# PEER products of a hybrid decoder block: 32 gated in PSUM and 16 kept in the rings of the split weights, gates stored for 32 tokens at a time

## The chip, the core and the metric

The kernel runs on one core of one Trainium2 chip. The metric is the device time of one execution in microseconds; the kernel before takes 1910.42 us, the median of three runs (1905.02 to 1913.4). Engines: TensorE (PE, its weight loads PEld), VectorE (DVE), ScalarE (ACT), GpSimd (POOL), SyncE (SP), and 16 DMA engines that serve the queues of SP, ACT and POOL.

## The reference

One decoder block for 512 tokens of width 1024: two token mixers (MLA attention and RWKV-7), merged by gates, then PEER, a mixture of 16384 experts, all in fp32. The change touches PEER alone:

```python
q = (h @ w_query).reshape(B, S, 8, 2, 128)
s1 = einsum('bshd,nd->bshn', q[..., 0, :], sub_keys1)      # 128 row keys
s2 = einsum('bshd,nd->bshn', q[..., 1, :], sub_keys2)      # 128 column keys
...                                                        # top 16 of each, then top 16 of their sums
expert_idx = i1 * 128 + i2                                 # 16 experts for each of 8 heads
gates = softmax(top_v)
act = gelu(einsum('bpd,bphkd->bphk', h_blk, expert_down[idx]))
out = einsum('bphk,bphkd->bpd', gates * act, expert_up[idx])
```

So a token has 128 experts of 16384. The result is x + gt2 * out.

## The kernel before

The 512 tokens are four blocks of 128. After the token mixers (RWKV in chunks, MLA, `tail_a` to `tail_c`, which end with the query products `ps_q`, the scores `ps_sc` and the selection `select`), the blocks go two ways. Blocks 0 and 1 are **gathered** (`peer`, L1141): for each of the 128 slots an indirect DMA of POOL brings one expert row for each token (`gl`, 128 x 2048, 1 MB, four buffers), VectorE makes the dot product with the token (`gl`, L1156), ACT the gelu and the gate (`z`), and VectorE adds the weighted second half to `acc` (L1163), one slot later, which frees the buffer. Between block 0 and block 1, `acc` is stored and cleared again by POOL.

Blocks 2 and 3 (256 tokens) are **dense**: all 16384 experts are computed for them, 128 at a time; i is the row key, 0 to 127. `dense_z(i)` (L1202) multiplies the 128 down weights `u_raw` with the tokens, 128 x 256 results, and applies the gelu. It has two forms. Made ahead of the loop, it takes the weights as they are, as eight fp32 products with `hf`, which the trace shows as 16 passes. In the loop it splits the weights into a high part `uh` (ACT) and a low part `ul` (VectorE) of a faster format and makes 24 products with the split tokens `hh` and `hl`. `uh` and `ul` have two buffers each.

Before the change 24 products (`AF_`) are made into `Af`, 8 more (up to `AZ` = 32) into a tile `A`, and 8 more (`PZ`) into `zp`, which ACT stores to DRAM as `zd`; the loop loads them again into the first slots of `Af`.

`dense_spread` (L1241) turns the selected experts into gates. For eight tokens (`HB`) VectorE makes one-hots of the row and column keys in 16-bit (`o`, four of 1024 elements at a time) and weights them with the gates (`og`); TensorE multiplies them (`ps_G`), which gives for each token a 128 x 128 table, four tokens in one PSUM bank. VectorE multiplies the first `AF_` rows straight into `Af` out of PSUM (L1290); ACT copies the other rows into `g_` (L1288), and one DMA of ACT's queue stores `g_` to DRAM as `gd` for every `TB` = 16 tokens (L1291). `g_` and the gate tiles `G` that the loop loads back share `NG` = 3 buffers. ahead["z"] is stepped once for each 16 tokens, so 16 products are made during the spread.

The loop of `dense` (L1314) goes over i. It loads the up weights `v_raw`, splits them (`vh`, `vl`), multiplies `act` by the gates `G` if i >= `AF_` (L1334), splits the product (`ch`, `cl`) and adds 12 products of 512 columns to four PSUM accumulators. `gates_of` loads `G` for eight rows i at a time. All products, copies and splits go through the helpers of L237 and L1187 to L1188.

What sets the order: the program is written stage by stage, and a scheduler gives each engine one fixed order by data readiness, a cost model and a priority. `tc.cur_priority += LATE` marks the gather steps and `ZLATE` the products made ahead as work for gaps. So the gathers of both blocks lie between the instructions of all stages from 470 us on.

Of the kernel before, what the change touches and what calls it, by code (L numbers as in the profile page):

```python
# [9 lines left out]
F32 = mybir.dt.float32  # L10
# [25 lines left out]
ZLATE = 100  # L36
ZFIRST = 24
AZ = 32
AF_ = 24
PZ = 8  # L40
NG = 3
BG = [[0.91, 2, 2, 1.0, 2.2, 2.85, 2.45, 1.0], [1.6, 2.28, 1, 0.58, 0.25, 0.5, 0.13, 0.36]]
# [114 lines left out]
def _build(ctx, tc, nc, A, out):  # L157
# [1017 lines left out]

    TB = 16
    HB = 8
# [3 lines left out]
    dn, ahead = {}, {}  # L1181
    zd = dp.tile([P, PZ, nd], F32, name="zd")
    NJ = P // SUB - AF_ // SUB
# [18 lines left out]
    def dense_z(i):  # L1202
# [3 lines left out]
        if i < AF_:  # L1206
            act = dn["first"][:, i]
        elif i < AZ:
            if i % SUB == 0:
                dn["A"] = dz.tile([P, SUB, nd], F32, name="A", tag="A", bufs=(AZ - AF_) // SUB)  # L1210
            act = dn["A"][:, i % SUB]
        elif i < AZ + PZ:
            act = dz.tile([P, nd], F32, name="zp", tag="zp", bufs=2)
        else:
            act = dn["v"].tile([P, nd], F32, name="act", tag="act", bufs=2)
        u = dz.tile([P, D], F32, name="u_raw", tag="u", bufs=4)
        nc.sync.dma_start(u, A["dense"][i, 0])
        if i < AZ + PZ:
            zs = ((u, dn["hf"]),)
# [10 lines left out]
        S.activation(act, ps[:, :nd], AF.Gelu_apprx_tanh)  # L1230
        if AZ <= i < AZ + PZ:
            nc.scalar.dma_start(zd[:, i - AZ], act)
        else:
            dn["act"][i] = act

    def dense_ahead():
        for i in range(AZ + PZ):
            dense_z(i)
            yield
# [54 lines left out]
    def dense(sel):  # L1294

        n = nd
        for _ in dense_spread(sel):
            step(ahead["z"])
        drain(ahead["z"])
# [14 lines left out]
        for i in range(P + 1):  # L1314
            if i < P:
                if i % SUB == 0:
                    if i >= AF_:
                        gates_of(i // SUB + NG - 1)
                    if AZ <= i + SUB < AZ + PZ:
                        t = dn["first"][:, i + SUB - AZ:i + 2 * SUB - AZ]  # L1320
                        nc.sync.dma_start(t, zd[:, i + SUB - AZ:i + 2 * SUB - AZ])
                        for j in range(SUB):
                            dn["act"][i + SUB + j] = t[:, j]
                if i >= AZ + PZ:
                    dense_z(i)
# [147 lines left out]
    for _ in streams[1]:  # L1473
        if "z" in ahead and nz < ZFIRST:
            tc.cur_priority += ZLATE
# [30 lines left out]
```

## Time and profile before

| what | before |
|---|---|
| median of three runs | 1910.42 us |
| the profiled execution | 1907.93 us, of which 1906.2 us is the span of the trace |
| TensorE busy | 1720.0 us (90%) |
| VectorE busy | 1587.9 us (83%) |
| ScalarE, GpSimd busy | 699.8 us (37%), 437.2 us (23%) |
| bytes moved | 588.75 MB, 309 GB/s over the span |

The stages of the end of the span: the last query scores are made by 1081 us, the selection of blocks 2 and 3 ends at 1126, the spread lasts from 1126 to 1247, the dense loop from 1248 to 1872, and the gathers of block 1 end at 1900. A timeline row gives start and duration in us, and in square brackets how long the engine stood idle before it and what ended that. [...]

### The profile page before, as it was taken

How to read it: one execution, taken by the hardware profiler on the slowest of the kernel's cores; microseconds unless marked ns; L12 is line 12 of the kernel's file. 1: busy time of each engine (PE TensorE's matmuls, PEld its weight loads, DVE VectorE, ACT ScalarE, POOL GpSimd, SP SyncE). 2: the span in 40 equal slices, each digit the busy share in tenths (PEclk: the TensorE clock that was granted, in tenths of full speed). 3: DMA queues.
4: the chain of work that ended last, by engine and by line, in shares of the span. 5: the costliest groups of instructions: out<-in, count | busy, mean ns of one | idle time of the engine just before them, and what ended most of it. 6: DMA issues, size and time to landing. Idle time of an engine off the chain costs nothing.

```text
span 1906.2 us, 30258 instructions
## 1 busy us (share of the span) xinstructions
PE 1720.0 (90%) x11018; PEld 1472.0 (77%) x11018; DVE 1587.9 (83%) x3654; ACT 699.8 (37%) x1727; POOL 437.2 (23%) x394
## 2 busy tenths in 40 slices
PE   5879999999899999999699979779999999999992
PEld 4667877778787698988388868657899988889892
DVE  4864446559778798888689999979999999999998
ACT  1233233321323232331131133335555555555551
POOL 1210010000222210222222222022333333333333
PEclk9889999999999999999899989879999999999996
DMA  9545654166986875889899889989999999999997
GB/s 385 196 154 172 230 174 161 44 217 204 365 333 211 345 247 190 298 312 362 330 351 351 317 302 316 293 330 399 400 403 416 415 416 415 414 408 415 411 373 281
DMA packets 146274, 588.75 MB, mean 309 GB/s; under 512 B 13886, under 2 KB 41918, under 8 KB 111564
## 3 DMA queue, kind: packets, MB, share of 16 engines
q1 hardware_dynamic: 76544, 284.69, 40.4%
q0 software_dynamic: 39360, 280.51, 38.2%
q10 hardware_dynamic: 30220, 21.60, 3.6%
q8 instruction: 87, 1.43, 0.3%
q14 instruction: 63, 0.52, 0.1%
HBM read 566.81 MB, written 19.94 MB: 308 GB/s over the span
## 4 chain that ended last, share of the span: by engine, by line
issue 31%; PE 31%; DVE 13%; POOL 12%; DMA 11%; ACT 1%; POOLq 0%; SPq 0%; ACTq 0%; DVEq 0%
POOL gl L1152 12%; DMA gl<-in_experts,ii 5%; PE ps_b L237 4%; PE ps_gt L237 4%; DMA w_b<-in_w_b 3%; PE ps_q L237 3%; DVE acc L1163 3%; PE ps_z L237 2%; DVE gl L1156 2%; PE ps_ap L237 2%; PE ps_y L237 1%; PE ps_m L237 1%; PE ps_G L237 1%; PE ps_M L237 1%; PE ps_s L237 1%
## 5 line engine op out<-in xcount | busy, mean ns | idle before, releaser
L1152 POOL DMA_INDIRECT gl<-in_experts,ii x256 | 382.9, 1496 | 989.1 <-DVE acc L1163 697.0
L1156 DVE SCALAR_TENSOR_TENSOR gl<-gl,h2p 128x1024 f32<-128x1024 f32 x256 | 311.3, 1216 | 49.8 <-DMA gl<-in_experts,ii 49.5
L1163 DVE SCALAR_TENSOR_TENSOR acc<-gl,z,acc 128x1024 f32<-128x1024 f32 x256 | 326.6, 1276 | 12.6 <-ACT z L1158 7.1
L237 PE MATMUL acc<-vl,ch 128*128 128x512 f32 x512 | 204.9, 400 | 7.4 <-DVE vl L1188 7.2
L237 PE MATMUL acc<-vh,cl 128*128 128x512 f32 x512 | 204.5, 399 | 5.0 <-DVE cl L1188 4.9
L237 PE MATMUL ps_z<-hh,uh 128*128 128x256 f32 x704 | 199.4, 283 | 0.0
L237 PE MATMUL ps_z<-hh,ul 128*128 128x256 f32 x704 | 199.4, 283 | 0.0
L237 PE MATMUL acc<-vh,ch 128*128 128x512 f32 x512 | 196.9, 397 | 2.7 <-ACT ch L1187 2.7
L237 PE MATMUL ps_z<-hl,uh 128*128 128x256 f32 x704 | 199.2, 283 | 0.0
L1157 ACT ACTIVATE z<-z 128x1 f32<-128x1 f32 x256 | 51.8, 203 | 368.0 <-DVE gl L1156 367.2
L237 PE MATMUL ps_z<-hf,u_raw 128*128 128x256 f32 x640 | 156.0, 388 | 8.4 <-ACT i1T L1264 8.4
L1188 DVE TENSOR_TENSOR vl<-v_raw,vh 128x1024 fp32r<-128x1024 f32 x128 | 156.0, 1219 | 4.6 <-ACT vh L1187 4.4
L237 PE MATMUL ps_gt<-hT,w_b 128*128 128x128 f32 x1024 | 136.9, 288 | 14.5 <-DMA w_b<-in_w_b 14.4
L237 PEld LDWEIGHTS ps_gt<-hT,w_b 128*128 128x128 f32 x1024 | 127.6, 201 | 20.9 <-DMA w_b<-in_w_b 11.5
L237 PEld LDWEIGHTS ps_z<-hl,uh 128*128 128x128 f32 x704 | 135.1, 192 | 3.8
L1187 ACT CAST vh<-v_raw 128x1024 fp32r<-128x1024 f32 x128 | 134.1, 1047 | 9.6 <-PE acc L237 4.8
L237 PEld LDWEIGHTS ps_z<-hh,uh 128*128 128x128 f32 x704 | 134.7, 191 | 3.4
L237 PEld LDWEIGHTS ps_z<-hh,ul 128*128 128x128 f32 x704 | 134.8, 191 | 0.3 <-DVE ul L1188 0.2
L237 PEld LDWEIGHTS ps_z<-hf,u_raw 128*128 128x128 f32 x640 | 117.1, 194 | 21.8 <-ACT i1T L1264 8.6
L237 PE MATMUL ps_b<-hT,w_b 128*128 128x128 f32 x896 | 123.6, 288 | 7.7 <-DMA w_b<-in_w_b 6.4
L237 PE MATMUL ps_q<-h2T,w_q 128*128 128x128 f32 x1024 | 125.6, 277 | 2.1 <-DMA w_q<-in_w_query 1.4
L237 PEld LDWEIGHTS ps_b<-hT,w_b 128*128 128x128 f32 x896 | 113.3, 200 | 18.0 <-DMA w_b<-in_w_b 6.3
(445 smaller groups left out, 3299.3 us busy)
## 6 DMA issues: line engine op xcount, KB each, us to landing
u_raw<-in_dense SPq DMA_DIRECT2D x128, 512.0 KB, 7.4
v_raw<-in_dense SPq DMA_DIRECT2D x128, 512.0 KB, 8.7
w_b<-in_w_b SPq DMA_DIRECT2D x82, 512.0 KB, 4.8
w_ada<-in_w_ada SPq DMA_DIRECT2D x48, 512.0 KB, 5.4
w_q<-in_w_query SPq DMA_DIRECT2D x48, 512.0 KB, 3.7
G<-gd SPq DMA_DIRECT2D x13, 1024.0 KB, 10.6
w_o<-in_w_o SPq DMA_DIRECT2D x24, 512.0 KB, 5.1
w_out<-in_w_out SPq DMA_DIRECT2D x24, 512.0 KB, 7.0
```

What stands on the lines that cost most here:

```text
L237: PE.matmul(o, l, r, start=start, stop=stop)
L1152: G.indirect_dma_start(out=gl, out_offset=None, in_=A["experts"], in_offset=bass.IndirectOffsetOnAxis(ap=ii[:, s:s + 1], axis=0))
L1156: V.scalar_tensor_tensor(gl[:, :D], gl[:, :D], 1.0, h2, op0=ALU.mult, op1=ALU.mult, accum_out=z[:, 0:1])
L1157: S.activation(z[:, 1:2], z[:, 0:1], AF.Gelu_apprx_tanh)
L1163: V.scalar_tensor_tensor(acc, gl[:, D:], z[:, 1:2], acc, op0=ALU.mult, op1=ALU.add)
L1187: S.copy(hi, x)
L1188: V.tensor_tensor(lo, x, hi.bitcast(F32), op=ALU.subtract)
```

## The change

`AF_` becomes 32, so `Af` has 32 rows and 32 rows of the gate table meet their products in PSUM; `A` and `AZ` go. The 16 products of i = 32 to 47 (`PZ`) go into tiles `zp` of four products each, which take the two `uh` buffers (32 to 39) and the two `ul` buffers (40 to 47); the loop reads them there, and `zd` goes. The first split weights of the loop are those of i = 48, which need `zp` read up to 43. `TB` becomes 32, `NG` 2, and `gd` has 12 groups of rows (`NJ`) and not 13, so 8 stores of 1536 runs of 1 KB take the place of 16 stores of 1664 runs of 512 B. ahead["z"] is stepped twice for each 32 tokens.

```diff
-ZFIRST = 24
-AZ = 32
-AF_ = 24
-PZ = 8
-NG = 3
+AF_ = 32
+PZ = 16
+NG = 2
...
-    TB = 16
+    TB = 32
...
-    zd = dp.tile([P, PZ, nd], F32, name="zd")
     NJ = P // SUB - AF_ // SUB
...
         if i < AF_:
             act = dn["first"][:, i]
-        elif i < AZ:
-            if i % SUB == 0:
-                dn["A"] = dz.tile([P, SUB, nd], F32, name="A", tag="A", bufs=(AZ - AF_) // SUB)
-            act = dn["A"][:, i % SUB]
-        elif i < AZ + PZ:
-            act = dz.tile([P, nd], F32, name="zp", tag="zp", bufs=2)
+        elif i < AF_ + PZ:
+            if i % 4 == 0:
+                tag = ("uh", "ul")[(i - AF_) // 8]
+                dn["zp"] = dz.tile([P, 4, nd], F32, name="zp", tag=tag, bufs=2)
+            act = dn["zp"][:, i % 4]
         else:
...
-        if i < AZ + PZ:
+        if i < AF_ + PZ:
             zs = ((u, dn["hf"]),)
...
-        if AZ <= i < AZ + PZ:
-            nc.scalar.dma_start(zd[:, i - AZ], act)
-        else:
-            dn["act"][i] = act
+        dn["act"][i] = act
...
         for _ in dense_spread(sel):
-            step(ahead["z"])
+            step(ahead["z"], 2)
...
-                    if AZ <= i + SUB < AZ + PZ:
-                        t = dn["first"][:, i + SUB - AZ:i + 2 * SUB - AZ]
-                        nc.sync.dma_start(t, zd[:, i + SUB - AZ:i + 2 * SUB - AZ])
-                        for j in range(SUB):
-                            dn["act"][i + SUB + j] = t[:, j]
-                if i >= AZ + PZ:
+                if i >= AF_ + PZ:
                     dense_z(i)
...
-        if "z" in ahead and nz < ZFIRST:
+        if "z" in ahead and nz < AF_:
```

The scheduler places everything anew from the end of the selection on; up to there VectorE's order is the same. At three places the orders are shown.

TensorE between the last scores (`ps_sc`) and the first gate table (`ps_G`); `ps_igT` are the transposes of the selection that the one-hots need, one row of `ps_z` is two passes in the trace. Before:

```order
L237 MATMUL ps_sc<-sk,qTp 128x128 x4
L237 MATMUL ps_z<-hf,u_raw 128x256 x71
L1263 MATMUL ps_igT<-cst,idx_8605 128x128
L237 MATMUL ps_z<-hf,u_raw 128x256 x3
L1263 MATMUL ps_igT<-cst,idx_8605 128x128
L237 MATMUL ps_z<-hf,u_raw 128x256 x4
L1263 MATMUL ps_igT<-cst,gates_8552 128x128
L237 MATMUL ps_z<-hf,u_raw 128x256 x6
L237 LDWEIGHTS o_8742
```

After:

```order
L235 MATMUL ps_sc<-sk,qTp 128x128 x4
L235 MATMUL ps_z<-hf,u_raw 128x256 x135
L1256 MATMUL ps_igT<-cst,idx_8604 128x128 x2
L235 MATMUL ps_z<-hf,u_raw 128x256
L1256 MATMUL ps_igT<-cst,gates_8551 128x128
L235 MATMUL ps_z<-hf,u_raw 128x256 x6
L235 LDWEIGHTS o_8837
```

The 64 products of eight more rows i stand ahead of the transposes.

VectorE at the start of the spread, from the last steps of the selection (`oh`, `idx`) to the first multiplication out of PSUM. Before:

```order
L1119 TENSOR_TENSOR oh<-oh 128x256
L1266 TENSOR_TENSOR gT<-gT,gb 128x128
L1120 TENSOR_TENSOR idx_8697<-oh 128x128
L1267 CAST gb<-gT 128x128
L1276 TENSOR_TENSOR o_8742<-iota,i2T 128x1024
L1276 TENSOR_TENSOR o_8743<-iota,i1T 128x1024
L1276 TENSOR_TENSOR o_8771<-iota,i2T 128x1024
L1279 TENSOR_TENSOR og<-o_8743,gb 128x1024 x2
L1163 SCALAR_TENSOR_TENSOR acc<-gl,z,acc 128x1024
L1276 TENSOR_TENSOR o_8772<-iota,i1T 128x1024
L1290 SCALAR_TENSOR_TENSOR Af<-Af,ps_G 128x24x4
```

After, from the same `oh` to the first one-hot (a seventh `gl` follows it, ahead of the first row of L1283):

```order
L1117 TENSOR_TENSOR oh<-oh 128x256
L1154 SCALAR_TENSOR_TENSOR gl,z<-gl,h2p 128x1024
L1118 TENSOR_TENSOR idx_8744<-oh 128x128
L1161 SCALAR_TENSOR_TENSOR acc<-gl,z,acc 128x1024
L1154 SCALAR_TENSOR_TENSOR gl,z<-gl,h2p 128x1024
L1161 SCALAR_TENSOR_TENSOR acc<-gl,z,acc 128x1024 x2
L1154 SCALAR_TENSOR_TENSOR gl,z<-gl,h2p 128x1024
L1161 SCALAR_TENSOR_TENSOR acc<-gl,z,acc 128x1024
L1154 SCALAR_TENSOR_TENSOR gl,z<-gl,h2p 128x1024
L1161 SCALAR_TENSOR_TENSOR acc<-gl,z,acc 128x1024
L1154 SCALAR_TENSOR_TENSOR gl,z<-gl,h2p 128x1024
```

Seven gathers moved ahead of the first gate. Counted over VectorE's whole order, 128 of the 256 `gl` stood ahead of the first `vl` before and 135 stand there now; behind the last `vl` there were 9 and are 6; the five `ul` of the spread are gone from it, and the first `ul` follows the 44th `vl`.

VectorE from the last multiplication out of PSUM to the first one by a loaded `G`, after the change (before, it read `Af`, `vl`, the end of block 0's `acc`, three `gl`, `acc` and four splits, and then `A<-A,G`):

```order
L1283 SCALAR_TENSOR_TENSOR Af<-Af,ps_G 128x32x4
L1185 TENSOR_TENSOR vl<-v_raw,vh 128x1024
L1161 SCALAR_TENSOR_TENSOR acc<-gl,z,acc 128x1024
L1154 SCALAR_TENSOR_TENSOR gl,z<-gl,h2p 128x1024 x2
L1185 TENSOR_TENSOR cl<-Af,ch 128x256
L1185 TENSOR_TENSOR vl<-v_raw,vh 128x1024
L1185 TENSOR_TENSOR cl<-Af,ch 128x256
L1161 SCALAR_TENSOR_TENSOR acc<-gl,z,acc 128x1024
L1154 SCALAR_TENSOR_TENSOR gl,z<-gl,h2p 128x1024
L1161 SCALAR_TENSOR_TENSOR acc<-gl,z,acc 128x1024
L1185 TENSOR_TENSOR vl<-v_raw,vh 128x1024
L1322 SCALAR_TENSOR_TENSOR zp<-zp,G 128x256
```

The end of block 0 (`acc<-acc,e`) moved from here into the spread.

## Rows read from the trace of the kernel before

**Rows 1.** Page, part 1: engine, busy us (share of the span), instructions.
```profile
PE 1720.0 (90%) x11018; PEld 1472.0 (77%) x11018; DVE 1587.9 (83%) x3654; ACT 699.8 (37%) x1727; POOL 437.2 (23%) x394
```
**Rows 2.** Two stretches: us, busy us of each engine, TensorE's clock, DMA, GB/s.
```profile
1250.00:1300.00 50.00, 41.91 (x153) 32.45 (x154) 38.25 (x63) 19.36 (x36) 8.65 (x6) 0.85 0.95 372
...
1500.00:1600.00 100.00, 99.70 (x637) 89.81 (x636) 98.07 (x131) 54.65 (x110) 34.52 (x21) 1.00 1.02 415
```
**Rows 3.** Waits from 1310 to 1870 us: us in total, times, longest.
```profile
POOL gl L1152 <- DVE acc L1163: 369.1, 111, 5.6
...
DVE gl L1156 <- DMA gl<-in_experts,ii: 6.5, 12, 1.2
```
**Rows 4.** TensorE's timeline in the dense loop: start us, duration us, instruction.
```profile
1500.45 0.40 PE L237 MATMUL acc<-vh,cl 128*128 128x512 f32 x1
1500.68 0.28 PE L237 MATMUL ps_z<-hh,uh 128*128 128x256 f32 x1
1500.80 0.28 PE L237 MATMUL ps_z<-hl,uh 128*128 128x256 f32 x1
```
**Rows 5.** VectorE's groups, 1310 to 1860 us: busy us, mean ns, idle before.
```profile
L1188 DVE TENSOR_TENSOR ul<-u_raw,uh 128x1024 fp32r<-128x1024 f32 x83 | 101.6, 1224 | 0.1
...
L1334 DVE SCALAR_TENSOR_TENSOR act<-act,G 128x256 f32<-128x256 f32 x84 | 34.9, 415 | 0.0
```
**Rows 6.** TensorE's timeline between the last scores and the spread.
```profile
1080.74 30.59 PE L237 MATMUL ps_z<-hf,u_raw 128*128 128x256 f32 x141
...
1124.74 4.49 PE L237 MATMUL ps_z<-hf,u_raw 128*128 128x256 f32 x12 [8.39 <-ACT i1T L1264]
```
**Rows 7.** VectorE's timeline: the first one-hot and the first gate.
```profile
1126.52 0.68 DVE L1276 TENSOR_TENSOR o<-iota,i2T 128x1024 f16<-128x1024 f16 x1
...
1131.33 0.24 DVE L1290 SCALAR_TENSOR_TENSOR Af<-Af,ps_G 128x96 f32<-128x96 f32 x1
```
**Rows 8.** POOL's and VectorE's timelines, two gathers: issue, then first use.
```profile
906.05 1.68 POOL L1152 DMA_INDIRECT gl<-in_experts,ii  x1 [4.07 <-DVE acc L1163]
...
915.53 1.23 DVE L1156 SCALAR_TENSOR_TENSOR gl<-gl,h2p 128x1024 f32<-128x1024 f32 x1 [3.74 <-DMA gl<-in_experts,ii]
...
1878.12 1.68 POOL L1152 DMA_INDIRECT gl<-in_experts,ii  x1 [6.21 <-DVE acc L1163]
...
1884.53 1.23 DVE L1156 SCALAR_TENSOR_TENSOR gl<-gl,h2p 128x1024 f32<-128x1024 f32 x1 [0.60 <-DMA gl<-in_experts,ii]
```
**Rows 9.** VectorE's groups, 1125 to 1250 us: the multiplications out of PSUM.
```profile
L1290 DVE SCALAR_TENSOR_TENSOR Af<-Af,ps_G 128x96 f32<-128x96 f32 x64 | 14.3, 246 | 2.9 <-ACT g__9404 L1288 1.7 <-ACT g__9700 L1288 0.4 <-ACT g__9774 L1288 0.4
```
**Rows 10.** Last gate store (op, ns, start), and SP's wait for it (total, times, longest).
```profile
L1291 ACTq DMA_DIRECT2D gd<-g__9848 x1: 521/521/521, 1246.9 to 1246.9; - x1
...
SPq L1307 <- DMA gd<-g__9848: 10.8, 1, 10.8
```
**Rows 11.** VectorE's timeline: last gate, and the loop's first waits.
```profile
1247.42 0.25 DVE L1290 SCALAR_TENSOR_TENSOR Af<-Af,ps_G 128x96 f32<-128x96 f32 x1
...
1260.36 1.28 DVE L1163 SCALAR_TENSOR_TENSOR acc<-gl,z,acc 128x1024 f32<-128x1024 f32 x1 [4.96 <-POOL acc L1147]
...
1266.37 0.43 DVE L1334 SCALAR_TENSOR_TENSOR A<-A,G 128x256 f32<-128x256 f32 x1 [3.25 <-DMA G<-gd]
1266.71 0.42 DVE L1188 TENSOR_TENSOR cl<-Af,ch 128x256 fp32r<-128x256 f32 x1
```
**Rows 12.** POOL's timeline: a gather's issue in the spread.
```profile
1213.87 4.42 POOL L1152 DMA_INDIRECT gl<-in_experts,ii  x1 [25.08 <-DVE Af L1290]
```
**Rows 13.** VectorE's timeline: the last `vl`, and the last gathers.
```profile
1865.28 1.22 DVE L1188 TENSOR_TENSOR vl<-v_raw,vh 128x1024 fp32r<-128x1024 f32 x1
1866.41 1.27 DVE L1163 SCALAR_TENSOR_TENSOR acc<-gl,z,acc 128x1024 f32<-128x1024 f32 x1
...
1895.58 1.28 DVE L1163 SCALAR_TENSOR_TENSOR acc<-gl,z,acc 128x1024 f32<-128x1024 f32 x1 [0.60 <-ACT z L1158]
...
1898.60 1.28 DVE L1163 SCALAR_TENSOR_TENSOR acc<-gl,z,acc 128x1024 f32<-128x1024 f32 x1 [0.60 <-ACT z L1158]
```

More of the change, by code (lines that the diff above doesn't have):

```diff
@@ L1230, in dense_z @@
         S.activation(act, ps[:, :nd], AF.Gelu_apprx_tanh)
-        if AZ <= i < AZ + PZ:
-            nc.scalar.dma_start(zd[:, i - AZ], act)
-        else:
-            dn["act"][i] = act
+        dn["act"][i] = act
     def dense_ahead():
-        for i in range(AZ + PZ):
+        for i in range(AF_ + PZ):
             dense_z(i)
```

## Prediction

> **What bounds the kernel now.** First the busy times: TensorE and VectorE hold 90% and 83% of the span [rows 1], so the stages have to be looked at one by one. The change works on the last 830 us. Cut into stretches, the dense loop runs with VectorE at 98.07 of 100 us, TensorE at 99.70 and the DMA engines full at 415 GB/s, while its first 50 us have VectorE at 38.25 of 50 and a granted TensorE clock of 0.85, a mean of time at 1.2 and at 2.4 GHz [rows 2]. Next, who waits for whom in that loop: the gathers on POOL wait 369.1 us for VectorE's `acc`, which frees their buffers, and VectorE waits only 6.5 us for gathered data [rows 3]. So VectorE is never without work there; DMA is full without yet being late. TensorE is no looser: a 512-column product starts 0.23 us after the one before it, a 256-column one 0.12 us [rows 4], so one round (12 of the first, 24 of the second) needs 12 x 0.23 + 24 x 0.12 = 5.64 us, and no gap stands between them. Last, the end: VectorE splits the last `vl` at 1865.28 and is busy with left-over gathers up to the last `acc` at 1898.60, 7.6 us before the span ends [rows 13]. VectorE's last gather ends the kernel, hence VectorE's work and its idle time from 1125 us on are the sum to make; TensorE is checked against it.
>
> **VectorE's work.** Eight products move from the split form to the fp32 form ahead of the loop. Each drops one `ul` of 1.22 us [rows 5]; the next instruction starts 0.08 us before such a one is over (1865.28 to 1866.41 [rows 13]), so 8 x 1.13 = 9.0 us go. Eight more groups of products (24 to 31) meet their gates in PSUM and drop the multiplication by `G`, 0.34 us from start to start (1266.37 is followed by 1266.71, as the 0.42 of [rows 5] less the same overlap): 8 x 0.34 = 2.7 us. Against that, the 64 multiplications out of PSUM grow from 96 to 128 elements. 96 take 246 ns [rows 9], 256 take 415 [rows 5]: 1.06 ns for an element, 64 x 32 x 1.06 = 2.2 us more. Work: -9.0 - 2.7 + 2.2 = **-9.5 us**. Gathers are only moved: one costs 1.14 + 1.20 = 2.34 us wherever it stands (a `gl` of 1.23 [rows 8] and an `acc` of 1.28 [rows 13], less the same overlap).
>
> **The start of the spread.** Before, VectorE goes from selection straight to the first one-hot at 1126.52 and the first gate at 1131.33 [rows 7]. The new order puts seven gathers ahead of the first gate, because 32 products must now be there and not 24. TensorE needs 30.59 / 141 = 0.217 us for a pass of an fp32 product, 16 passes = 3.47 us, and 8 more are 27.8 us; it stood idle for 8.39 us at this place [rows 6], the rest lies beside VectorE's seven gathers (7 x 2.34 = 16.4 us). The products are thus hidden; were the cover gone, each would cost 3.47. What I charge is the wait for gathered data. Four buffers exist, and two full ones stand ready. The third gather can start only when the first `acc` frees a buffer, near 1127. Where gathers stood close together, one issued at 906.05 was waited for until 915.53, 9.5 us; at the quiet end, issued at 1878.12, it was there at 1884.53, 6.4 us [rows 8]. With 9.5 us VectorE waits until 1136.7 though it would be ready near 1133, and the next ones follow at 2.5 to 3.5 us: 5 us lost. If the products' weights (0.52 MB per 3.47 us, 150 GB/s) leave only 265 of 415 GB/s, a gather of 1.05 MB takes 4 us and 9 us are lost. With 6.4 us almost nothing is. I take **+7**, between the two readings of the crowded row that it resembles; bounds 0 and 12.
>
> **Inside the spread.** VectorE idled 2.9 us before its PSUM multiplications, for ACT's copies of `g_` [rows 9]. ACT loses five `uh` casts, eight stores of `zp` and half of its gate stores there, so I take **-2**; at best -2.9, and the other end is the rival below.
>
> **The start of the loop.** VectorE lost 4.96 us to the clearing of `acc` behind the store of the first gathered block, and 3.25 us to the first `G` [rows 11]. The seven gathers let the first block end inside the spread, so the first wait goes. What is late next: in the new order two `gl` and one `acc` stand directly behind the spread, and the second `gl` has its buffer freed only 5 us ahead: with 9.5 us to land it waits 4. The first `G` has to wait for the last store, which was issued at 1246.9 and made the load queue wait 10.8 us [rows 10]. That store has 1536 runs now (1664 before), of 1 KB and not 512 B. Priced by runs it takes as long as before, and VectorE, whose order reaches the `G` some 16 us after the last gate (18.95 before, 1247.42 to 1266.37 [rows 11]), waits 1 to 5 us; by bytes (x1.85) the 14.6 us from issue to release become 27, and it waits 16. Queued behind that wait are the `v_raw` loads on SP and the first `cl`. I take runs: **0** for this place in all, bounds -8 and +11.
> On this the Trainium skill's "DMA: Bandwidth & Descriptors" (Queues, rings and completion order) says that an engine serves the queues in turn, a packet at a time; by that rule the run count decides beside busy queues. No row separates runs from bytes, as all stores here are alike.
>
> The Trainium skill's "SBUF — State Buffer" (SBUF: two separate sides) says that GpSimd cannot write gather descriptors while VectorE holds the shared port in a two-port mode. Its trace sign is here: a gather's issue on POOL takes 4.42 us beside the 16-bit one-hots [rows 12] and 1.68 away from them [rows 8]. By the rule a gather wanted right behind the spread lands 2.7 us later still, which would turn the 0 of the last step into +3.
>
> **The end.** Behind the last `vl` the order has three gathers fewer. In that tail every `gl` and `acc` pair waits about 0.6 us for ACT between them (one gather in 3.02 us, 1895.58 to 1898.60 [rows 13]), so three gathers fewer are up to 3 x 0.6 = 1.8 us of waits fewer; **-1.5**, bounds -3 and +2 (a landing of 9.5 and not 6.4 us there [rows 8]).
>
> **Sum**: -9.5 + 7 - 2 + 0 - 1.5 = -6.0 us. The profiled execution took 1907.93 us around a span of 1906.2; it lies 2.5 below the median 1910.42. So 1901.9 for such an execution, **1904** for a median (-0.3%). TensorE's check: its loop falls from 128 x 2.76 + 85 x 2.88 = 598 us (three split products were made in the spread) to 128 x 2.76 + 80 x 2.88 = 584, and starts later by 16.4 + 7 less what the spread saves (five `ul` of 1.13, 2.0 of idle, 2.2 back, 5.5 in all), 18 us. It would end 4 us later, with three gathers of 3 us fewer behind it: -5. The two ways agree.
>
> **Rivals.** (a) *The work comes through whole.* The DMA load falls (2 MB of `zd`, 2 MB of gates, 14,000 runs), gathers land in the 6.4 us of the quiet row, and the vanished 4.96 us are not replaced: -9.5 + 1 - 2.9 - 4 - 1.5 = -17, so 1893; with half of it 1899. For it: VectorE waits 6.5 us for data in a loop with DMA full [rows 3], so data is rarely late. Against it: [rows 8], where gathers stand as close as they will. (b) *The two gate buffers bind, slower.* Group g+2 of 32 tokens copies into the buffer of group g, whose store must be over: some 14.5 us of time, as long as three buffers of 16 tokens gave. Priced by bytes a store takes 27 us in company; VectorE's gate needs ACT's copy [rows 9], so six groups wait. It decides from 14.5 us a store; at 18 it costs 6 x 3.5 = 21 and 5 at the loop's start, -6 + 26 = +20: 1930. Against it: three buffers were enough under a fuller DMA, and with runs the price is nil. (c) *The change does not remove the stall it moves.* The products wait in the rings of `uh` and `ul`, so the first split waits for product 43 and the loop starts on split products with none in hand, where five `ul` were done by the spread's end. If TensorE, as tight as VectorE [rows 2], has to wait there for three rounds' products (3 x 2.88 = 8.6), the time is 1910 to 1913.
>
> **Chances.** About 0.5%, 9.6 us, is what a measurement of this kernel can tell from no change. The forecast 1901 to 1908: 0.44; (a) 1889 to 1900: 0.36; (b) 1920 to 1940: 0.12; (c): 0.08. Faster 0.36, same 0.51 (forecast and most of (c)), slower 0.13. The range 1890 to 1915 leaves out most of (b) and the far edge of (a).
>
> **What would show it.** `ul` 80 times and the multiplications by `G` 96 times; the PSUM ones near 0.28 us. The first one-hot near 1146 and the first gate near 1153; waits of 5 to 9 us for gathers ahead of it. No wait of ACT for `gd`. The last gate near 1265, no wait on POOL's clearing of `acc`, the first `G` with a wait of 1 to 5 us. The last `vl` near 1867 and 6 gathers behind it. I am wrong by (a) if the waits before the first gate are under 2 us, by (b) if ACT's copies wait for stores, by (c) if TensorE idles where `act` begins.

## The result and the profile after

The changed kernel takes 1895.1 us (median of ten runs, 1887.16 to 1899.35) against 1910.0 (ten runs, 1898.86 to 1913.4): a ratio of 0.9922, 95% interval 0.9903 to 0.9942. It is faster by 0.8%, some 15 us. The forecast was 1904 with a range of 1890 to 1915: the time lies inside, the sign is right, and the gain is two and a half times the 6 us that were worked out.

| | before | after |
|---|---|---|
| the profiled execution, and its span | 1907.93, 1906.2 us | 1887.16, 1885.4 us |
| TensorE busy | 1720.0 us | 1715.8 us |
| VectorE busy | 1587.9 us | 1577.7 us |
| bytes moved | 588.75 MB | 584.53 MB |

The line of the page on busy times, after (as [rows 1] before):

```profile
PE 1715.8 (91%) x10954; PEld 1467.6 (78%) x10954; DVE 1577.7 (84%) x3638; ACT 690.7 (37%) x1719; POOL 422.8 (22%) x394
```

The spans differ by 20.8 us and the medians by 14.9. The cast of `iota`, an instruction of VectorE at the selection's end, up to which both orders are the same, starts at 1125.11 before and at 1118.38 after; 6.7 us thus lie ahead of the change. A second profiled execution of the changed kernel has it at 1130.49. So everything below is measured from that cast. From there to the end of the span it is 781.09 us before, and 767.02 and 768.61 in the two executions after: 14.1 and 12.5 us fewer, which agrees with the medians.

Stretches of VectorE's time: from the cast to the first gate, the spread, from the last gate to the first multiplication by `G`, from there to the last `vl`, the tail. The columns are us, then busy us of PE, PEld, DVE, ACT and POOL, TensorE's clock, DMA share, GB/s. Before:

```profile
1125.11:1131.33 6.22, 6.22 (x34) 5.12 (x34) 6.22 (x15) 1.06 (x3) 0.26 (x1) 0.76 0.61 193
1131.33:1247.42 116.09, 99.38 (x811) 84.42 (x809) 112.28 (x221) 43.96 (x103) 25.46 (x9) 0.91 0.94 303
1247.42:1266.37 18.95, 13.06 (x37) 9.10 (x37) 10.60 (x17) 7.52 (x18) 4.30 (x3) 0.73 0.90 322
1266.37:1865.28 598.91, 591.79 (x3517) 521.41 (x3518) 586.87 (x783) 327.46 (x644) 194.69 (x116) 0.99 1.01 405
1865.28:1906.20 40.92, 5.85 (x24) 3.87 (x22) 33.30 (x44) 5.64 (x22) 12.47 (x8) 0.63 0.77 280
```

After:

```profile
1118.38:1147.90 29.52, 22.24 (x103) 18.13 (x102) 23.31 (x37) 6.44 (x24) 8.57 (x7) 0.83 0.90 365
1147.90:1258.20 110.30, 94.45 (x745) 78.56 (x743) 107.39 (x213) 37.78 (x96) 11.16 (x10) 0.86 0.78 279
1258.20:1276.30 18.10, 11.31 (x35) 8.09 (x36) 11.99 (x18) 6.14 (x16) 4.29 (x3) 0.70 1.01 365
1276.30:1855.00 578.70, 574.15 (x3402) 507.31 (x3401) 571.80 (x760) 322.53 (x631) 190.04 (x112) 1.00 1.01 406
1855.00:1885.40 30.40, 5.62 (x23) 3.69 (x21) 24.73 (x33) 3.30 (x14) 7.06 (x4) 0.69 0.70 259
```

The reader is to take from each row its length less DVE's busy time, which is VectorE's idle time there: 0, 3.8, 8.4, 12.0 and 7.6 us before (31.8 in all), 6.2, 2.9, 6.1, 6.9 and 5.7 after (27.8). VectorE's work from the cast on is 749.3 us before and 739.2 after. The gain of 14.1 us is 10.0 us of work and 4.0 of idle time.

VectorE's timeline at the start of the spread, after (start, duration, instruction, in brackets the idle time and what ended it):

```profile
1128.41 1.23 DVE L1154 SCALAR_TENSOR_TENSOR gl<-gl,h2p 128x1024 f32<-128x1024 f32 x1 [1.74 <-DMA gl<-in_experts,ii]
...
1130.24 1.28 DVE L1161 SCALAR_TENSOR_TENSOR acc<-gl,z,acc 128x1024 f32<-128x1024 f32 x1 [0.60 <-ACT z L1156]
...
1132.80 1.23 DVE L1154 SCALAR_TENSOR_TENSOR gl<-gl,h2p 128x1024 f32<-128x1024 f32 x1 [1.27 <-DMA gl<-in_experts,ii]
...
1140.32 1.23 DVE L1154 SCALAR_TENSOR_TENSOR gl<-gl,h2p 128x1024 f32<-128x1024 f32 x1 [0.65 <-DMA gl<-in_experts,ii]
1141.47 0.08 DVE L1154 DVE_READ_ACCUMULATOR gl<-gl,h2p 128x1 f32 x1
1141.47 0.69 DVE L1269 TENSOR_TENSOR o<-iota,i1T 128x1024 f16<-128x1024 f16 x1
```

The gathers moved ahead are waited for in small pieces: 4.3 us for their data and three times 0.6 for ACT's gate between `gl` and `acc`. The same view at the loop's start, after (as [rows 11] before):

```profile
1263.40 1.23 DVE L1154 SCALAR_TENSOR_TENSOR gl<-gl,h2p 128x1024 f32<-128x1024 f32 x1 [1.29 <-DMA gl<-in_experts,ii]
...
1270.26 1.23 DVE L1154 SCALAR_TENSOR_TENSOR gl<-gl,h2p 128x1024 f32<-128x1024 f32 x1 [2.62 <-DMA gl<-in_experts,ii]
...
1276.30 0.42 DVE L1322 SCALAR_TENSOR_TENSOR zp<-zp,G 128x256 f32<-128x256 f32 x1 [2.14 <-DMA G<-gd]
...
1283.54 0.42 DVE L1185 TENSOR_TENSOR cl<-Af,ch 128x256 fp32r<-128x256 f32 x1 [1.19 <-ACT ch L1184]
```

The wait for the clearing of `acc` is gone, the second gather is waited for in its place, and the wait for `G` is a little shorter.

### The profile page after: what moved, and what is told of

Read it like the earlier page. It is cut to its first block, busy times and chain, and to the rows that moved or that the text cites. A ratio compares the mean times of both kernels' runs of the same rounds, so it can differ in the third digit from the quotient of the medians.

```text
span 1885.4 us, 30072 instructions
## 1 busy us (share of the span) xinstructions
PE 1715.8 (91%) x10954; PEld 1467.6 (78%) x10954; DVE 1577.7 (84%) x3638; ACT 690.7 (37%) x1719; POOL 422.8 (22%) x394
## 2 busy tenths in 40 slices
DMA packets 130369, 584.53 MB, mean 310 GB/s; under 512 B 13598, under 2 KB 26270, under 8 KB 95916
## 4 chain that ended last, share of the span: by engine, by line
PE 32%; issue 27%; DVE 15%; DMA 14%; POOL 12%; ACT 1%; SPq 0%; POOLq 0%; DVEq 0%; ACTq 0%
POOL gl L1150 12%; DMA gl<-in_experts,ii 6%; PE ps_b L235 4%; PE ps_gt L235 4%; PE ps_q L235 3%; DMA w_b<-in_w_b 3%; DMA w_ada<-in_w_ada 3%; PE ps_ap L235 3%; DVE gl L1154 2%; DVE acc L1161 2%; PE ps_y L235 1%; PE ps_z L235 1%; PE ps_m L235 1%; PE ps_sq L235 1%; DVE og L1272 1%
## 5 line engine op out<-in xcount | busy, mean ns | idle before, releaser
L1150 POOL DMA_INDIRECT gl<-in_experts,ii x256 | 368.4, 1439 | 997.8 <-DVE acc L1161 707.4
L1161 DVE SCALAR_TENSOR_TENSOR acc<-gl,z,acc 128x1024 f32<-128x1024 f32 x256 | 326.3, 1275 | 6.1 <-ACT z L1156 5.4
L235 PE MATMUL ps_z<-hf,u_raw 128*128 128x256 f32 x768 | 185.0, 388 | 3.9 <-DMA u_raw<-in_dense 3.9
L235 PE MATMUL ps_z<-hh,ul 128*128 128x256 f32 x640 | 181.1, 283 | 0.0
L235 PE MATMUL ps_z<-hh,uh 128*128 128x256 f32 x640 | 181.0, 283 | 0.0
L235 PE MATMUL ps_z<-hl,uh 128*128 128x256 f32 x640 | 181.0, 283 | 0.0
L235 PEld LDWEIGHTS ps_z<-hf,u_raw 128*128 128x128 f32 x768 | 141.2, 193 | 20.8 <-issue 4.5
L235 PE MATMUL ps_gt<-hT,w_b 128*128 128x128 f32 x1024 | 132.7, 283 | 12.9 <-DMA w_b<-in_w_b 12.7
L235 PEld LDWEIGHTS ps_q<-h2T,w_q 128*128 128x128 f32 x1024 | 122.1, 192 | 4.6 <-ACT h2T L1022 1.5
L235 PEld LDWEIGHTS ps_z<-hl,uh 128*128 128x128 f32 x640 | 122.9, 192 | 3.5
L235 PEld LDWEIGHTS ps_z<-hh,uh 128*128 128x128 f32 x640 | 122.5, 191 | 3.1
## 6 DMA issues: line engine op xcount, KB each, us to landing
G<-gd SPq DMA_DIRECT2D x12, 1024.0 KB, 10.4
```

The source lines that it names most:

```text
L235: PE.matmul(o, l, r, start=start, stop=stop)
L1150: G.indirect_dma_start(out=gl, out_offset=None, in_=A["experts"], in_offset=bass.IndirectOffsetOnAxis(ap=ii[:, s:s + 1], axis=0))
L1161: V.scalar_tensor_tensor(acc, gl[:, D:], z[:, 1:2], acc, op0=ALU.mult, op1=ALU.add)
```

## Experiments

From here on theory V says that the end is set by VectorE's work from the cast on plus its waits; its rivals put the end down to TensorE's rounds, to the DMA engines, or to the gate buffers. All runs in one table: the ratio to the kernel before, run on the same chip (medians 1909.8 to 1911.2), with its interval, and from one profiled execution each, the time from the cast to the end of the span, VectorE's work in it, and its idle time. Work and idle time add up to the time in any kernel; that they do is no evidence for V.

| kernel | products ahead | median us | ratio | cast to end | work | idle |
|---|---|---|---|---|---|---|
| before | 40 | 1910.0 | 1 | 781.1 | 749.3 | 31.8 |
| changed | 48 | 1895.1 | 0.9922 [0.9903, 0.9942] | 767.0 | 739.2 | 27.8 |
| changed_again | 48 | 1899.3 | 0.9926 [0.9900, 0.9952] | 768.6 | 740.3 | 28.3 |
| gates_only | 40 | 1923.7 | 1.0079 [1.0047, 1.0111] | 796.3 | 750.1 | 46.2 |
| gates_early | 40 | 1926.3 | 1.0081 [1.0054, 1.0107] | 791.0 | 750.2 | 40.8 |
| af24 | 40 | 1908.7 | 0.9986 [0.9960, 1.0012] | 778.0 | 749.3 | 28.6 |
| pz8 | 40 | 1908.9 | 0.9997 [0.9972, 1.0023] | 781.7 | 749.2 | 32.6 |
| no_gates | 48 | 1912.4 | 1.0005 [0.9980, 1.0030] | 782.8 | 740.6 | 42.2 |
| no_gates_late | 48 | 1906.8 | 0.9979 [0.9950, 1.0009] | 782.2 | 740.6 | 41.7 |
| igt_first | 48 | 1903.3 | 0.9964 [0.9937, 0.9992] | 777.5 | 740.5 | 37.0 |
| u5 | 48 | 1893.1 | 0.9903 [0.9874, 0.9931] | 766.2 | 739.9 | 26.4 |
| pz20 | 52 | 1889.8 | 0.9900 [0.9862, 0.9937] | 762.9 | 734.9 | 27.9 |
| less_pe | 48 | 1911.7 | 1.0006 [0.9983, 1.0030] | 787.8 | 741.6 | 46.2 |
| more_dma | 48 | 1932.7 | 1.0122 [1.0073, 1.0171] | 766.4 | 739.8 | 26.6 |

**The parts alone.** gates_only is the kernel before with the stores of the change:

```diff
-NG = 3
+NG = 2
-    TB = 16
+    TB = 32
-            step(ahead["z"])
+            step(ahead["z"], 2)
```

> The kernel before with only the gate stores changed: 32 tokens a store, two buffers, 8 stores of 1 KB runs; products and split weights as before. Theory V (the end is VectorE's work plus its waits): VectorE's work stays the same, only its waits for ACT's copies can shrink, so about 1909 us (1905 to 1912), ratio to before 0.997 to 1.001. Theory D (the DMA engines' time decides): half the runs are gone, q10 falls from about 35% to 25% of the engines' time in 135 us, so up to 13 us are gained: 1897 to 1902. Theory B (two gate buffers bind): ACT's copies wait for stores, 1920 or more, and the trace shows it.

It came out at 1923.7, slower than before by 0.8%. Theory V as put here and theory D both missed; B's number came, but hardly by its mechanism: ACT waits once for a gate buffer, 4.8 us, and VectorE waits for ACT's copies for 0.9 us in all. VectorE's work is that of before, and the idle time grew by 14.4 us, most of it at one place, as its timeline at the loop's start shows:

```profile
1258.63 1.23 DVE L1156 SCALAR_TENSOR_TENSOR gl<-gl,h2p 128x1024 f32<-128x1024 f32 x1 [10.37 <-DMA h2p<-h2d]
...
1271.71 1.22 DVE L1169 TENSOR_TENSOR acc<-acc,e 128x1024 f32<-128x1024 f32 x1
...
1288.55 1.23 DVE L1156 SCALAR_TENSOR_TENSOR gl<-gl,h2p 128x1024 f32<-128x1024 f32 x1 [7.87 <-DMA gl<-in_experts,ii]
```

The order that the scheduler makes with the new stores has the end of block 0 (`acc<-acc,e`) among the loop's first rounds. There VectorE waits 10.4 us for the next block's `h2p` and 7.9 for a gather, which POOL could issue only when `acc` was done. Before the change the end of block 0 stood at the end of the spread and cost 4.96 us [rows 11]; in the changed kernel it stands inside the spread (1168 to 1175) and costs nothing that shows.

no_gates is the other part alone, the changed kernel with the old stores:

```diff
-NG = 2
+NG = 3
-    TB = 32
+    TB = 16
-            step(ahead["z"], 2)
+            step(ahead["z"])
```

> The changed kernel with the gate stores put back to 16 tokens, three buffers and 512-byte runs (12 groups kept); 48 products ahead as in the change. Theory V: within 2 us of the changed kernel, 1895 to 1898, ratio to before 0.992 to 0.994. Theory D: the runs come back, 1900 to 1905. The last store has as many runs as the changed kernel's (1536), so by runs it holds back the first G for about 13 us as there, by bytes for about half of that.

1912.4: no gain at all is left, and both V's 1895 to 1898 and D's 1900 to 1905 missed. The work is the changed kernel's (740.6), the idle time is 42.2 and not 27.8. Of these 14 us, 12 lie between the first `G` and the last `vl` (19.0 for 6.9), where VectorE waits 10.6 us for gathers (4.9 in the changed kernel) and 7.0 for `vh` (0.4). The longest of the latter, in VectorE's timeline:

```profile
1317.02 1.23 DVE L1185 TENSOR_TENSOR vl<-v_raw,vh 128x1024 fp32r<-128x1024 f32 x1 [4.14 <-ACT vh L1184]
```

and what ACT waited for, in its own:

```profile
1315.95 1.04 ACT L1184 CAST vh<-v_raw 128x1024 fp32r<-128x1024 f32 x1 [4.09 <-DMA v_raw<-in_dense]
```

The third thing expected here missed too. The last store has the 1536 runs of the changed kernel's and half its bytes; by runs it was to hold back the first `G` for some 13 us, by bytes for half of that. From its issue to the first load of `G` it was 4.8 us, and 4.7 in no_gates_late:

```profile
1270.19 0.52 ACTq L1284 DMA_DIRECT2D gd<-g__9932  x1
1274.95 0.81 SPq L1300 DMA_DIRECT2D G<-gd  x2
```

Beside it the DMA engines moved 0.13 MB. Beside the last store of the changed kernel it was 3.1 MB, most of it gathers, and 4.1 before.

So alone the stores cost 0.8%, alone the products bring nothing, and together they bring 0.8%: the parts don't add up.

pz8 and af24 take the eight more products away in the two possible places:

```diff
-PZ = 16
+PZ = 8
```

> The changed kernel with 40 products ahead, not 48: products 40 to 47 take the split form again, all else as in the change. Theory V: 8 more ul of 1.13 us each, +9.0: 1904 us (1901 to 1907), ratio 0.996. Theory D says about the same (4.2 MB move back into a loop that runs at 406 GB/s, +10). Theory T (TensorE's products decide): 8 x 2.88 in place of 8 x 3.47 us, -4.7: 1890.

```diff
-AF_ = 32
+AF_ = 24
```

> The changed kernel with 24 products gated in PSUM, not 32, and 16 in the rings: 40 products ahead. VectorE's order has no gathers ahead of the first one-hot, as before the change. Theory V: +9.0 for 8 ul, +2.7 for 8 multiplications by G, -2.2 out of PSUM, -6.2 for the idle time at the spread's start, +5 for the wait on the clearing of acc that comes back: 1903 us (1899 to 1907), ratio 0.996. If the idle time at the spread's start has nothing to do with the eight more PSUM products: 1909, ratio 0.999.

1908.9 and 1908.7, where V had said 1904 (1901 to 1907) and 1903 (1899 to 1907), and T 1890 for the first: V missed both by some us. The work is up by 9 to 10 us in both, as the sum of `ul` and gates has it; in pz8 idle time is up by 4 to 5 us beside it. In af24 the idle time at the spread's start is gone, as expected, and comes back at the loop's start (a gather is waited for 7.6 us at once); so 1909, the number of the other reading, came without its reason. T's 1890 did not come, but pz8 says little against T: TensorE is busy 717.2 us from the cast on, 707.8 and 709.5 in the two executions of the changed kernel, since fewer of its products stand ahead of the cast. Nor does it part V from D, which had asked for the same.

**The same kernel again, and the place of the block's end.** changed_again is the changed kernel on the chip of the next three runs.

> The changed kernel again, beside the next three on one chip, as their measure: 1895 us, ratio to before 0.990 to 0.994. If the 0.8% was a matter of the chip and not of the change, the ratio comes out above 0.997.

0.9926: the gain is the change's. gates_early is gates_only with the last gathers of block 0 moved up:

```diff
-    for _ in dense([sel[b] for b in DENSE]):
-        tc.cur_priority += LATE
+    for n, _ in enumerate(dense([sel[b] for b in DENSE])):
+        late = -3000 if n < 66 else LATE
+        tc.cur_priority += late
         step(gather)
-        tc.cur_priority -= LATE
+        tc.cur_priority -= late
```

> gates_only with one thing more: the last gathers of block 0 get a higher priority, so that the change of blocks (end of acc, its store, clearing, load of the next h2p) falls inside the spread and not behind the loop's first rounds. Theory S (where the change of blocks falls sets 18 us: in gates_only VectorE waits 10.4 us for h2p and 7.9 for the gather behind it): 1923 less some 15 to 18, 1905 to 1909, ratio 0.997 to 1.000. Theory B (gate stores in two buffers are what costs, as little as the trace shows of it): 1920 or more.

1926.3, no gain; theory S falls as the whole explanation. The profiled execution is the fastest of the six, 1915.9, so the trace shows less than the median's loss. The waits at the loop's start did go (VectorE idles 13 us less from the last gate to the 48th round), but 12 us came up in the spread, and the medians are equal. ACT's waits in the spread (total us, times, longest) and VectorE's timeline there:

```profile
ACT zp L1230 <- DMA zd<-zp: 14.7, 2, 13.8
...
ACT g__9026 L1288 <- DMA gd<-g__8741: 5.9, 1, 5.9
```

```profile
1194.19 0.25 DVE L1290 SCALAR_TENSOR_TENSOR Af<-Af,ps_G 128x96 f32<-128x96 f32 x1 [8.30 <-ACT g__9168 L1288]
```

ACT cannot write the next `zp` before an earlier one is stored, and that store (issued at 1173.89) stands in ACT's queue behind a gate store of 1.7 MB (issued at 1171.81). Behind the waiting `zp` ACT's copies of `g_` queue up, and VectorE's gates behind these. So with `zd` still there a large store can block a small one. It need not: in gates_only, with the same stores, ACT waits 1.3 us for `zd`, and its loss lies elsewhere. af24, which has the same gate stores and the same 40 products but keeps `zp` in the rings, has 12 to 18 us less idle time than these two, and is as fast as the kernel before.

**The wait at the spread's start.** igt_first writes eight products behind the first transposes, u5 gives `u_raw` a fifth buffer:

```diff
-        if "z" in ahead and nz < AF_:
+        if "z" in ahead and nz < AF_ - 8:
...
                 V.tensor_copy(gb[:, 1, tb], gT[:, tb])
+                if q == 0:
+                    step(ahead["z"], 8)
```

> The changed kernel with eight of the 32 products ahead of the first gate written behind the transposes of the selection: one-hots can begin at once, gathers stand between them and not ahead of them. Theory G (VectorE's 6.1 us at the spread's start are waits for gathered data that stands too close together): part of it is filled by one-hots, 1890 to 1895, ratio 0.989 to 0.992. Theory T (TensorE's eight products are what the first gate waits for there): VectorE's waiting only changes its name, from gathers to the first gate, 1895 to 1900.

```diff
-        u = dz.tile([P, D], F32, name="u_raw", tag="u", bufs=4)
+        u = dz.tile([P, D], F32, name="u_raw", tag="u", bufs=5)
...
-        gt2 = dn["z"].tile([P, D], F32, name="gt2", tag="u", bufs=4)
+        gt2 = dn["z"].tile([P, D], F32, name="gt2", tag="u", bufs=5)
```

> The changed kernel with five buffers for u_raw, not four; VectorE's order is the same. TensorE waited 3.9 us for a u_raw load among the gathers ahead of the first gate. Theory G: VectorE reaches its one-hots later than TensorE its products, nothing changes: 1894 to 1897, ratio 0.991 to 0.993. Theory T: up to 3.9 us fewer, 1891.

igt_first took 1903.3, slower than either theory had it. The one-hots came at once, but TensorE waited 8.4 us for `i1T` ahead of the eight products, the first gate came 10 us later from the cast on (39.8 against 29.5), and VectorE's waits around the gathers grew, 7.3 us for their data and 2.4 for ACT's gate between the first one-hot and the first gate. u5 changed nothing that can be told apart from the changed kernel (766.2 against 767.0 and 768.6 from the cast): its first gate stands 29.5 us behind the cast as in the changed kernel, though TensorE no longer waits there for `u_raw`. The 3.9 us were not on VectorE's path.

**The loads at the loop's start.** no_gates_late lets no_gates load `G` one group ahead and not two:

```diff
-        for j in range(NG - 1):
+        for j in range(1):
...
-                        gates_of(i // SUB + NG - 1)
+                        gates_of(i // SUB + 1)
```

> no_gates (48 products ahead, stores of 16 tokens in 512-byte runs, three buffers, 1912 us) with the loads of G one group ahead and not two, as the changed kernel has it; VectorE's order is that of no_gates. Theory L (no_gates loses its time to v_raw loads that come late behind one more 1 MB load of G at the loop's start, 4.1 us of waiting at once): 1902 to 1906, ratio 0.995 to 0.998. Theory R (the 512-byte runs of the stores cost it): 1910 to 1914, ratio above 0.999.

The median, 1906.8, lies between the two forecasts, the ratio, 0.9979, at the edge of L's, and its interval overlaps that of no_gates. The trace says more: 782.2 from the cast to the end against 782.8, idle 41.7 against 42.2, and the longest wait for `vh` is still there, 3.8 us for 4.1. So the one more load of `G` is not what makes `v_raw` late. What makes no_gates idle 14 us longer than the changed kernel, most of it in waits for loads and gathers inside the loop, stays open.

**What bounds the end.** pz20 makes four more products ahead:

```diff
-PZ = 16
+PZ = 20
...
-                tag = ("uh", "ul")[(i - AF_) // 8]
-                dn["zp"] = dz.tile([P, 4, nd], F32, name="zp", tag=tag, bufs=2)
+                tag = ("uh", "ul", "zx")[(i - AF_) // 8]
+                dn["zp"] = dz.tile([P, 4, nd], F32, name="zp", tag=tag, bufs=1 if tag == "zx" else 2)
```

> The changed kernel with four more products ahead (52), in one more tile of 4 KB. Theory V (each is worth one ul): 4 x 1.13 = 4.5 us fewer, 1892, ratio 0.990. Theory T (each is worth its 2.88 us on TensorE, as TensorE has gaps at the spread's end for them): 11.5 us fewer, 1885, ratio 0.987. By the step that was measured from 40 to 48 products (11 to 14 us for eight), 1890.

1889.8; by the trace 4.1 to 5.7 us fewer than the changed kernel from the cast on, with 4.3 to 5.4 us less work. That is V's 4.5 and not T's 11.5. The median is the 1890 of the measured step; its interval overlaps that of the changed kernel, and only the profiled stretch separates the two. V and D are not parted here either: four `u_raw` fewer in the loop are 2.1 MB, some 5 us at the 406 GB/s of the loop. less_pe takes 77 us of products off TensorE:

```diff
-            zs = ((uh, hh_), (uh, hl_), (ul, hh_))
+            zs = ((uh, hh_), (ul, hh_))
```

> The changed kernel without one of the three terms of the split products (uh with hl): 80 x 8 products of 0.12 us, 77 us of TensorE's loop, are left out; VectorE's work is the same, and 32 more gathers are left for the time behind the loop. Theory T (TensorE's rounds set the end): 1830 to 1850. Theory V (VectorE's work sets it, and gathers that don't fit a shorter loop come behind it): 1890 to 1915, the tail longer by what the loop is shorter.

1911.7: T falls, V's range holds. The last `vl` came 78 us sooner (658.5 us behind the cast, 736.6 in the changed kernel), and the tail took it back and 20 us more. The stretches there (columns as above), and VectorE's waits for ACT between `gl` and `acc` (total us, times, longest):

```profile
1750.00:1800.00 50.00, 38.47 (x221) 33.31 (x219) 49.41 (x68) 22.58 (x47) 18.84 (x10) 0.92 0.87 329
1800.00:1850.00 50.00, 0.00 (x0) 0.00 (x0) 39.81 (x51) 8.45 (x34) 28.14 (x17) 0.50 0.99 359
1850.00:1900.00 50.00, 0.00 (x0) 0.00 (x0) 40.45 (x50) 7.95 (x32) 25.35 (x16) 0.50 0.98 347
```

```profile
DVE acc L1161 <- ACT z L1156: 22.7, 38, 0.6
```

TensorE has nothing to do for the last 100 us and more while VectorE works off 32 more gathers than in the changed kernel, each with its 0.6 us of waiting; for their data it waits only 0.5 us there, so the end is VectorE's (with ACT's part of each gather) and not the DMA engines', at 0.98 of their time. What sets the loop's length this run does not say: with the 32 gathers the scheduler also took some 75 us of VectorE's work and 34 MB out of the loop, and VectorE is as full there as TensorE. For the changed kernel's loop the trace shows that VectorE does not wait on DMA for long (4.9 us of 578.7 for gathers), while the loads wait for it to free their buffers, most of all those of `v_raw` (SP's waits from 1276 to 1855 us: total, times, longest):

```profile
SPq L1316 <- DVE vl L1185: 235.2, 97, 4.7
```

more_dma adds loads that nobody reads:

```diff
                 if i >= AF_ + PZ:
                     dense_z(i)
+                    if i % 3 == 0:
+                        xx = dn["z"].tile([P, D], F32, name="xx", tag="xx", bufs=1)
+                        nc.sync.dma_start(xx, A["dense"][i - 1, 0])
```

> The changed kernel with 27 extra loads of 0.5 MB in the loop (14.2 MB that nobody reads), on VectorE the same order. At 415 GB/s they take 34 us of the DMA engines. Theory D (the loop goes by the DMA engines, which show 1.02 of their time busy): 25 to 34 us more, about 1925. Theory V: VectorE's waits for gathered data grow by a few us at most, 1896 to 1902.

1932.7, near D's number, and yet no word on the loop. Nothing in the loop reads `xx`, and the scheduler put all of the loads far ahead (operation, ns, first and last start):

```profile
L1316 SPq DMA_DIRECT2D xx<-in_dense x27: 327/328/432, 910.7 to 1075.0; - x27
```

There the one buffer of `xx` made each load wait in SP's queue for the one before, and the loads of `w_q` and `w_out` behind them came late for TensorE (waits from 905 and from 940 us to 1165):

```profile
SPq L1316 <- DMA xx<-in_dense: 142.9, 26, 21.3
```

```profile
PE ps_q L235 <- DMA w_q<-in_w_query: 29.7, 5, 10.9
```

In the changed kernel TensorE has no such wait. From the cast on the kernel is the changed one (766.4); the cast itself comes at 1164.72. Whether the loop, with its DMA engines at 1.02 of their time, would bear more bytes was thus not tried.

## Why the prediction was right, and where it was not

**VectorE's work: right.** -9.5 forecast, -10.0 and -9.0 in the two executions. Over the table the work is 749 to 750 us with 40 products ahead, 739 to 742 with 48 and 735 with 52, whatever the order. The counts came as announced, VectorE's groups after, 1125 to 1870 us (busy us, mean ns, idle before):

```profile
L1185 DVE TENSOR_TENSOR ul<-u_raw,uh 128x1024 fp32r<-128x1024 f32 x80 | 97.7, 1221 | 0.0
L1322 DVE SCALAR_TENSOR_TENSOR act<-act,G 128x256 f32<-128x256 f32 x80 | 33.0, 413 | 0.0
L1283 DVE SCALAR_TENSOR_TENSOR Af<-Af,ps_G 128x128 f32<-128x128 f32 x64 | 16.3, 279 | 1.5 <-ACT g__9846 L1281 0.7 <-ACT g__9703 L1281 0.6
L1322 DVE SCALAR_TENSOR_TENSOR zp<-zp,G 128x256 f32<-128x256 f32 x16 | 6.1, 418 | 2.1 <-DMA G<-gd 2.1
```

**The start of the spread: right in size, +6.2 for +7.** The make-up was another: no wait of 4 us for the third gather but four waits of 0.65 to 1.74, and 0.6 for ACT three times, which the estimate had not counted; that the two come to the same size is luck. The first one-hot stands 23.1 us behind the cast (announced 1146, that is 21 behind it), the first gate 29.5 (28), the last gate 139.8 (140), the last `vl` 736.6 (742).

**Inside the spread: -0.9 for -2.** ACT's copies are still waited for near its end.

**The loop's start up to the first `G`: -2.2 for 0.** The parts were seen rightly (gathers 3.9 us for an estimated 4, `G` 2.1 us for 1 to 5). From the last store's issue to the first load of `G` it was 14.6 us with 1664 runs before (1246.86 to 1261.49) and 13.8 with 1536 now, 0.94 times for 0.92 times the runs and 1.85 times the bytes. So the 27 us by bytes did not come. But a price by runs alone is not shown either: the same 1536 runs took 4.8 us in no_gates, with hardly anything beside them, so what stands beside the store weighs more than its runs. That the forecast priced it right rests on like company in the two kernels. The rows, store and load:

```profile
L1284 ACTq DMA_DIRECT2D gd<-g__9846 x1: 521/521/521, 1257.6 to 1257.6; - x1
```

```profile
1271.37 0.33 SPq L1300 DMA_DIRECT2D G<-gd  x1
```

**Behind the first `G`: -5.1 where the sum had next to no term. This is the step that failed.** The 0 for "the start of the loop" took in the `v_raw` loads and the first `cl` behind the wait for `G` without a price for them, and from there to the last `vl` VectorE's idle time was taken to stay at its 12.0 us. It fell to 6.9, and to 5.3 to 6.7 in the three other executions with this order of VectorE (changed_again, u5, more_dma). Counted to the loop's start, the 0 would be -7.3, near the end of its bounds of -8 and +11. VectorE's waits for `vh` alone went from 4.4 us to 0.4. From 1125 us on, before and then after:

```profile
DVE vl L1188 <- ACT vh L1187: 4.4, 6, 1.9
```

```profile
DVE vl L1185 <- ACT vh L1184: 0.4, 2, 0.2
```

Two of those six waits before, 1.89 and 0.57 us, stand behind a slow piece of TensorE. It stood idle for 3.03 us behind VectorE's wait for the first `G`, and went on at 1.2 GHz, the lower of its two levels (granted clock 0.51 from 1270 to 1275): one product of 512 columns each 0.43 us and not 0.23, up to 1274.7. TensorE's timeline before, at that place:

```profile
1268.99 0.80 PE L237 MATMUL acc<-vl,ch 128*128 128x512 f32 x1 [3.03 <-DVE vl L1188]
1269.58 0.63 PE L237 MATMUL acc<-vh,cl 128*128 128x512 f32 x1
1270.01 0.63 PE L237 MATMUL acc<-vh,ch 128*128 128x512 f32 x1
...
1275.25 0.39 PE L237 MATMUL acc<-vl,ch 128*128 128x512 f32 x1
1275.47 0.40 PE L237 MATMUL acc<-vh,cl 128*128 128x512 f32 x1
```

ACT then waited for it, and VectorE for ACT's `vh` behind that, the two timelines before:

```profile
1273.66 0.40 ACT L1187 CAST ch<-Af 128x256 fp32r<-128x256 f32 x1 [6.77 <-PE acc L237]
```

```profile
1275.16 1.23 DVE L1188 TENSOR_TENSOR vl<-v_raw,vh 128x1024 fp32r<-128x1024 f32 x1 [1.89 <-ACT vh L1187]
```

After, the idle time ahead of it is 1.91 us and the slow piece lasts from 1278.9 to 1282.4, and VectorE waits 1.2 us for it (the last row on the loop's start above). So the slow clock can account for some 1.3 us of the 5.1, 2.5 before less 1.2 after. This is read from the two traces; no run took the slow clock alone away. The other four waits for `vh` before (0.29, 0.25, 0.32 and 1.07 us, from 1296 to 1321) came at a granted clock of 1.00. Ahead of the first three ACT waited for a load of `v_raw`, ahead of the last for VectorE's own `cl`; ACT's rows ahead of the first and the last:

```profile
1295.35 1.05 ACT L1187 CAST vh<-v_raw 128x1024 fp32r<-128x1024 f32 x1 [1.28 <-DMA v_raw<-in_dense]
...
1319.22 1.05 ACT L1187 CAST vh<-v_raw 128x1024 fp32r<-128x1024 f32 x1 [1.13 <-DVE cl L1188]
```

Why these are gone after stays open. The other pieces of the 5.1 are the 0.8 us for the load of `zd`, which no longer exists, and 1.6 us less for gathers, against 1.3 more for `ch`.

**The end: -1.9 for -1.5**, with six gathers behind the last `vl`, as counted.

Together -10.0 + 6.2 - 0.9 - 2.2 - 5.1 - 1.9 = -13.9 us of the 14.1 (the rest is rounding) against -6.0. So the likeliest case, 1901 to 1908, did not come. The time lies where rival (a) had put it, 1889 to 1900, but not by (a)'s way: (a) wanted the gathers at the spread's start to be on time, and they cost what the forecast had charged.

**TensorE's check agreed with the sum for no good reason.** It gave -5 and was taken as a second way. less_pe shows that time taken off TensorE alone does not come off the end; both engines were full in the loop, and a sum on the one could come near a sum on the other without being a second proof.

**Rival (b)** did not decide here: in the changed kernel ACT never waits for a store. Its mechanism is real, though: ACT waited 4.8 us for a gate buffer in gates_only, 3.7 in af24 and 5.9 in gates_early, and 13.8 there for a small store behind a large one, which (b) had not thought of. What keeps the changed kernel clear of the latter is the part that looked unrelated, `zp` in the rings: it has no small stores. The sum had priced the parts one by one and could not see that. **Rival (c)** did not show: TensorE is busy for 99.99 of 100 us from 1300 and 100.00 from 1400 on, across the first `act`.

On the Trainium skill's two rules: "DMA: Bandwidth & Descriptors" (Queues, rings and completion order) has an engine serve the queues in turn, a packet at a time. The last store agrees with it as far as it took 13.8 and 14.6 us beside gathers and 4.8 alone; no run here separates a turn by packets from another way of sharing. By "SBUF — State Buffer" (SBUF: two separate sides) the gather behind the spread was to land 2.7 us later than charged; the waits for the two gathers there were 1.29 and 2.62 us, and the gathers issued last ahead of them (1256.82 and 1261.24) took 0.94 and 1.68 us to issue and not 4.42, so no run here shows it.

## What to carry to other kernels

Work taken off the engine that sets the end could be counted here to a microsecond from the rows, over all orders; idle time could not: with the work of 48 products ahead and TensorE's work unchanged it was 26 to 42 us, and with 40 it was 29 to 46, depending on the static order. So the sum should have a term for every stretch in which that engine idles, also behind the first wait of a loop, and the range should come from there. Parts of a change that share a queue or one scheduled order are to be tried together, since alone they may even have the other sign. An experiment that adds loads has to say what they wait for and what stands behind them, or it measures its own queue. And a trace is best compared from a common instruction just ahead of the change: run to run the cast moved by 12 us, the 768 us behind it by 1.6.

## What the runs showed of the hardware that was not expected

- 27 loads of 0.5 MB that nothing reads, put between 910 and 1075 us, moved the selection by 34 us or more (cast at 1164.72; 1118.38 to 1130.49 in the other executions). It need not be their bytes: the stage moves 336 GB/s with them and 328 in the changed kernel, and 415 elsewhere. What the trace shows is SP's queue waiting 142.9 us for one `xx` after the other, and TensorE waiting 38 us for `w_q` and `w_out` from the same queue.
- A store of 128 KB in ACT's queue, issued 2.1 us behind a gate store of 1.7 MB, held ACT up for 13.8 us in gates_early; with stores of the same sizes it was 1.3 us in gates_only.
- A store of 1536 runs took 4.8 us from issue to the release of its reader with 0.13 MB moved beside it, and one of 1536 runs of twice the length 13.8 us with 3.1 MB beside it.
- Gathers one after another, with TensorE idle, take 3.02 us each on VectorE, 0.6 of it waiting for ACT; less_pe shows it over some 38 of them (`acc` at 1840.92, 1843.95, 1846.97 and so on).
